# Mixture-of-experts stage: the partner rows of a group's remainder tile are fetched one expert later

## The chip, the cores and the metric

One core of a Trainium2 chip runs the whole program. The metric is the device time of one execution in microseconds (us). A core has five engines that each run their own instruction queue in order and wait for each other by semaphores: TensorE (PE), VectorE (DVE), ScalarE (ACT), GpSimd (POOL) and SyncE (SP). SP and POOL also issue DMA transfers.

## The reference, cut to what matters

One encoder layer over 2048 tokens of width 1024: an input projection, a state-space mixer beside a cross-attention, an output projection, a layer norm, and a mixture of experts with a second layer norm. The change lies in the mixture of experts. Each token picks one of 4 groups and in it 2 of 4 experts; an expert is a gated feed-forward network of width 256.

```python
def _hier_moe(x, wg, bg, we, be, w_gate, w_up, w_down):
    ...
    gsel = jnp.argmax(gl, axis=-1)
    ...
    top_v, top_i = lax.top_k(el, MOE_TOPK)
    ew = jax.nn.softmax(top_v, axis=-1) * gw
    eid = gsel[:, None] * MOE_EXPERTS_PER_GROUP + top_i
    gate = jnp.sum(jax.nn.one_hot(eid, MOE_EXPERTS, dtype=f32) * ew[..., None], axis=1)
    h = jax.nn.silu(jnp.einsum('td,edf->tef', t, w_gate)) * jnp.einsum('td,edf->tef', t, w_up)
    y = jnp.einsum('tef,efd->td', h * gate[..., None].astype(h.dtype), w_down)
...
        moe = _hier_moe(x, router_g_w[i], ...)
        x = _layer_norm(DEEPNORM_ALPHA * x + moe, ln2_g[i], ln2_b[i])
```

## The kernel before, in words

The stages ahead of the experts take the first 690 us or so. Then 16 experts run, in 4 groups of 4, in the order 0 to 14, one overflow tile (named `s0`, for rows that found no place), 15. An expert e handles 288 rows: 256 as two tiles of 128 rows, `xg{e}_0` and `xg{e}_1`, and 32 remainder rows. The remainder rows of the 4 experts of a group g share one tile of 128 rows, `xr{g}`.

What happens to a tile, with the names and lines of the profile:

- `fetch`: SP loads the expert's three f32 weight blocks into `raw` (three buffers); ScalarE (`L91`) and VectorE (`L92`) split each into a high and a low f16 part, `wh` and `wl`. POOL gathers the rows of the two tiles from `x1d` in memory by an indirect DMA (`L1201`).
- `columns`: PE transposes the rows (`pt`, `L1458`), ScalarE copies the high part (`xh`, `L1461`), VectorE takes the low part (`xl`, `L1462`).
- `hidden`: gate and up matmuls `pg`, `pu` (three f16 products each, `L108` to `L110`), two halves; `gated` (`L1046` to `L1049`) makes `hh` on ScalarE and `hl` on VectorE.
- `down`: the down matmuls into `py` (three PSUM buffers in all); VectorE adds `py` times the gate into the tile (`L1499`), which frees the PSUM buffer.
- `store` (`L1206`): POOL scatters the tile into a scratch `xs` in memory, so that the token's other expert finds the sum so far. `earlier` (`L1222`): POOL fetches that sum from `xs`.
- `finish`: the layer norm (`norm`) and a scatter to the output (`L1242`).

The remainder rows end apart: `rest_downs(g)` runs their down matmuls, ScalarE copies the result to `gyr{g}`, VectorE adds it into `xr{g}` (`L1518`), POOL stores `xr{g}`. `partner` then fetches the rows' sums from `xs` into `pzr{g}` (one of two buffers `pz`), and `finish` runs `L881` (`pzr` + `gyr`, VectorE), the square (`L886`, ScalarE), `L882` and `L887` (small, VectorE), the power (`rsr`, `L898`, POOL), `L900` and `L901` (VectorE) and the scatter.

In the loop over the experts (`for n_, e in enumerate(order)`) one iteration writes: the fetches for the next expert, the first half of `hidden(e)`, `downs` of the expert before, `columns` of the next, the second half of `hidden(e)`, the `earlier` of this expert's tiles, and then two or three `finish` taken from the front of the list `todo`. So `downs(e)` is written in the iteration of the expert behind e.

What sets the order on the engines: a scheduler reads the program in written order with its dependencies and sorts each engine's instructions by its own model of their times; on the chip each engine runs its list in order. A fetch from `xs` waits for all stores to `xs` that are written ahead of it; stores among themselves, and a store behind a fetch, don't wait. Tiles take their buffers from pools, `xg` and `gyr` from one of nine.

Of the kernel before, what the change touches and what calls it, by code (L numbers as in the profile page):

```python
# [18 lines left out]
P = 128  # L19
# [9 lines left out]
NE = 16  # L29
# [43 lines left out]
class Kern:  # L73
# [1176 lines left out]
    def moe(self):  # L1250
        nc, a = self.nc, self.a
        V = nc.vector
        with ExitStack() as m:
# [13 lines left out]
            rem = self.mk.tile([P, 4, LW], I32, bufs=1, name="idxrem")  # L1267
# [6 lines left out]
            def fetch_overflow(rows, i, nm, static=True):  # L1274
                li = self.mk.tile([P, 2], I32, tag="li", name=f"li{nm}")
                V.tensor_copy(li, rows[:, ds(i, 1)])
                tk = self.mk.tile([OVT, LW], I32, tag="tk", name=f"tk{nm}")
                with self.tc.issue_after(first) if static else ExitStack():
                    self.gather(tk, self.listd, li[:OVT, 0:1])
                W = self.expert_weights(lambda o, s: self.gather(o, s, li[:, 1:2]), nm)  # L1280
                xg = self.mk.tile([P, D], F32, tag="xg", bufs=XG, name=f"xg{nm}")
                self.gather(xg[:OVT], self.x1d, tk[:, 0:1])
                return W, xg, tk
# [4 lines left out]
            def overflow(f, h, nm):  # L1288
                W, xg, tk = f
                gy = self.gated_rows(nm)  # L1290
                self.down(W, *h, 0, OVT, xg, tk.bitcast(F32)[:OVT, 1:2], nm, gy=gy)
                return gy
# [21 lines left out]
            todo = []  # L1314

            def downs(e, W, xg, h):
                if e >= NE:
                    over.append(overflow(W, h, f"s{e - NE}"))
                    return
                g, i = divmod(e, 4)  # L1320
                hh, hl = h
                if e == NE - 1:
                    rest_downs(g)
                if e < EARLY:
                    x = self.xk[e]
                    if i:
                        todo.append((x, self.partner(P, idx[:, e, 0, 2:3], f"{e}_0"), None))
                        x = self.mk.tile([P, D], F32, tag="xg", bufs=XG, name="xg1_0")
                        self.gather(x, self.x1d, idx[:, e, 0, 0:1])
                        V.tensor_tensor(x, x, self.xk[e], op=ALU.add)  # L1330
                    with self.tc.issue_after(first):
                        self.store(x, P, idx[:, e, 0, 3:4])
                for q, (c, x) in enumerate(xg):
                    sums = [self.mk.tile([P, 1], F32, tag=f"sum{h}", bufs=6, name=f"sum{h}_{e}_{c}") for h in range(2)] if i else None
                    self.down(W, hh, hl, q * P, P, x, gate[:, e, c, 1:2], f"{e}_{c}", sums)
                    self.store(x, P, idx[:, e, c, 3:4])
                    if i:
                        todo.append((x, (None, idx[:, e, c, 2:3], f"{e}_{c}"), sums))
                if i == 3:
                    if e < NE - 1:  # L1340
                        rest_downs(g)
                    todo.append((gys.pop(g), self.partner(P, rem[:, g, 2:3], f"r{g}"), None))

            def rest_downs(g):
                left, xr = lefts.pop(g)
                gy = gys[g] = self.gated_rows(f"r{g}")
                self.down_rest(g, left, xr, gy, grem[:, g, 1:2])
                self.store(xr, P, rem[:, g, 3:4])
# [10 lines left out]
            lefts, rests, gys, over, before = {}, {}, {}, [], None  # L1359
# [7 lines left out]
            for n_, e in enumerate(order):  # L1367
                g, i = divmod(e, 4)
# [16 lines left out]
                if before is not None:  # L1385
                    downs(*before)
# [14 lines left out]
                for _ in range(3 if i == 1 else 2):  # L1401
                    if todo:
                        z, pair, sums = todo.pop(0)
                        self.finish(z, pair, HOW2, sums=sums)
                before = e, W, xg, h
            downs(*before)
            todo.append((over[0], self.partner(OVT, fo[2][:, 2:3], "s0"), None))
            for z, pair, sums in todo:
# [7 lines left out]
            with self.tc.If(flag != 0):  # L1416
# [3 lines left out]
                with self.tc.For_i(NSTAT, n, 1) as i:  # L1420
                    f = fetch_overflow(rows, i, "d", False)
# [170 lines left out]
```

## Time and profile before

| what | value |
|---|---|
| median of three runs | 1093.28 us |
| lowest and highest run | 1093.13, 1101.6 us |
| profiled execution | 1091.53 us |
| its span in the trace | 1089.7 us |
| PE busy over the span | 899.5 us (83%) |
| DVE, ACT, POOL busy | 828.3, 540.5, 535.3 us |

The span runs from the first to the last instruction in the trace; "busy" is the time in which an engine executes. A row of a timeline has the start, the duration, the engine, the line, the operation, the operands and, in brackets, how long the engine stood idle just before and what ended that.

### The profile page before, as it was taken

Reading aid. Unit: us, or ns where it says so; the run is one execution under the profiler, and the core shown is the slowest. Engines: PE = TensorE matmul, PEld = TensorE weight load, DVE = VectorE, ACT = ScalarE, POOL = GpSimd, SP = SyncE. Lnnn points to the kernel's source line nnn. Section 1 sums busy time; section 2 is a strip of 40 time slices with the busy share of each in tenths; the row PEclk is TensorE's granted clock in tenths of the full one; section 3 lists DMA queues with packets and bytes.
Section 4 is the critical chain, followed back from the end, with each engine's and each line's share of the span. In section 5 each row is a group of like instructions: output and inputs, shape, how many; then the busy total and the mean of one; then the engine's idle time right before and its main releaser. Section 6 shows DMA issues by size and latency. Waiting matters only on the chain. (4 is left out here: it accounts for less than half of the span.)

```text
span 1089.7 us, 18757 instructions
## 1 busy us (share of the span) xinstructions
PE 899.5 (83%) x7108; PEld 606.8 (56%) x7108; DVE 828.3 (76%) x1636; ACT 540.5 (50%) x1068; POOL 535.3 (49%) x379
## 2 busy tenths in 40 slices
PE   7777599985845999899999888698979987989880
PEld 4444465674734877444554447476657754755540
DVE  7999888969997666483585676467878787878774
ACT  5122243445748776477633312265656554746530
POOL 1475655426663331325945444525444566367454
PEclk9899799999887999999999987899999998999995
DMA  7113355275271422417736331476578669557531
GB/s 253 41 45 117 121 180 202 69 243 168 61 227 46 132 81 77 140 55 267 257 141 116 78 114 64 142 292 227 206 269 319 215 225 334 198 205 233 208 107 65
DMA packets 65199, 178.14 MB, mean 163 GB/s; under 512 B 15121, under 2 KB 33425, under 8 KB 57681
## 3 DMA queue, kind: packets, MB, share of 16 engines
q1 hardware_dynamic: 44800, 128.83, 36.2%
q0 software_dynamic: 20304, 48.07, 12.9%
q8 instruction: 57, 0.93, 0.3%
q14 instruction: 38, 0.30, 0.1%
HBM read 141.95 MB, written 58.49 MB: 184 GB/s over the span
## 5 line engine op out<-in xcount | busy, mean ns | idle before, releaser
L92 DVE SCALAR_TENSOR_TENSOR wl<-raw,wh 128x1024 f16<-128x1024 f32 x82 | 97.8, 1219 | 10.4 <-ACT wh L91 7.9
L91 ACT ACTIVATE wh<-raw 128x1024 f16<-128x1024 f32 x82 | 82.0, 1048 | 24.1 <-PE pg L109 13.8
L109 PE MATMUL pg<-xl,wh 128*128 128x288 f16 (+1 forms) x256 | 73.3, 288 | 3.0 <-DVE xl L1462 2.8
L110 PE MATMUL pg<-xh,wl 128*128 128x288 f16 (+1 forms) x256 | 73.3, 288 | 0.9 <-issue 0.9
L108 PE MATMUL pu<-xh,wh 128*128 128x288 f16 (+1 forms) x256 | 71.8, 283 | 2.4 <-DVE hl L1049 1.9
L108 PE MATMUL pg<-xh,wh 128*128 128x288 f16 (+1 forms) x256 | 73.5, 289 | 0.0
L1206 POOL DMA_INDIRECT xs<-xg,idxall x31 | 38.9, 1256 | 70.2 <-DVE xg L1499 40.9
L110 PE MATMUL pu<-xh,wl 128*128 128x288 f16 (+1 forms) x256 | 71.6, 282 | 1.5 <-issue 1.5
L109 PE MATMUL pu<-xl,wh 128*128 128x288 f16 (+1 forms) x256 | 71.6, 282 | 0.0
L109 PEld LDWEIGHTS <-wh 128*128 128x128 f16 x576 | 58.1, 101 | 19.0 <-issue 5.7
L108 PEld LDWEIGHTS <-wh 128*128 128x128 f16 x576 | 58.3, 101 | 18.5 <-issue 3.5
L110 PEld LDWEIGHTS <-wl 128*128 128x128 f16 x576 | 57.9, 101 | 17.5 <-issue 4.4
L108 PE MATMUL pq<-xh,S 128*128 128x128 f16 x256 | 51.0, 235 | 15.9 <-DVE OT L295 15.9
L743 POOL TENSOR_TENSOR pe<-pe,ri 128x1024 f32<-128x1024 f32 x16 | 30.3, 1895 | 55.5 <-DVE ri L742 38.8
L108 PE MATMUL pu<-winh,xh 128*128 128x512 f16 x128 | 49.7, 388 | 6.6 <-ACT winh L91 6.6
L1201 POOL DMA_INDIRECT xg<-x1d,idxall x31 | 37.9, 1222 | 32.9 <-DMA out_x<-xg,idxall 13.0
L108 PE MATMUL py<-wh,hh 128*128 128x512 f16 x120 | 45.9, 385 | 8.8 <-ACT hh L1048 4.6
L1462 DVE TENSOR_TENSOR xl<-pt,xh 128x512 f16<-128x512 f32 x60 | 39.5, 683 | 16.1 <-ACT xh L1461 10.1
L1461 ACT ACTIVATE xh<-pt 128x512 f16<-128x512 f32 x60 | 34.0, 592 | 35.8 <-PE pt L1458 29.5
L110 PE MATMUL pq<-xh,S 128*128 128x128 f16 x256 | 51.2, 235 | 0.4 <-DVE S L92 0.3
L1458 PE MATMUL pt<-ident,xg 128*128 128x128 f32 x240 | 37.8, 285 | 16.5 <-DVE xl L1462 7.6
L691 POOL TENSOR_TENSOR m<-S,R 128x1024 f32<-128x1024 f32 x10 | 30.4, 3045 | 42.0 <-DVE S L715 23.6
(471 smaller groups left out, 3163.6 us busy)
## 6 DMA issues: line engine op xcount, KB each, us to landing
raw<-in_w_gate SPq DMA_DIRECT2D x16, 1024.0 KB
raw<-in_w_up SPq DMA_DIRECT2D x16, 1024.0 KB
raw<-in_w_down SPq DMA_DIRECT2D x16, 1024.0 KB
xr<-in_xT SPq DMA_DIRECT2D x16, 512.0 KB
xs<-wo SPq DMA_DIRECT2D x16, 512.0 KB
wol<-xs SPq DMA_DIRECT2D x16, 512.0 KB
M<-kd SPq DMA_DIRECT2D x64, 128.0 KB
xres<-in_x SPq DMA_DIRECT2D x16, 512.0 KB
```

Of the source, the lines that this page charges most:

```text
L91: self.nc.scalar.activation(hi, raw, AF.Copy, scale=WS)
L92: self.nc.vector.scalar_tensor_tensor(lo, raw, WS, hi, op0=ALU.mult, op1=ALU.subtract)
L108: mm(ps, lh, rh, start=first, stop=False)
L109: mm(ps, lh, rl, start=False, stop=False)
L110: mm(ps, ll, rh, start=False, stop=last)
L691: Q.tensor_tensor(m[:, 1], S[:, :, 1::-1], tab(1), op=ALU.mult)
L743: nc.gpsimd.tensor_tensor(pe, pe, ri.unsqueeze(2).to_broadcast([P, 4, 256]), op=ALU.mult)
L1201: return self.nc.gpsimd.indirect_dma_start(out=out, out_offset=None, in_=src, in_offset=bass.IndirectOffsetOnAxis(ap=idx, axis=0))
L1206: st = self.nc.gpsimd.indirect_dma_start(out=self.xs, out_offset=bass.IndirectOffsetOnAxis(ap=si, axis=0), in_=z[:sz], in_offset=None, bou ...
L1458: nc.tensor.transpose(pt[:, i, off:off + sz], x[:sz, (d0 + i) * P:(d0 + i) * P + P], self.ident[:sz, :sz])
L1461: nc.scalar.activation(xh[:, ds_, :n], pt, AF.Copy)
L1462: nc.vector.tensor_tensor(xl[:, ds_, :n], pt, xh[:, ds_, :n], op=ALU.subtract)
```

## The change

In `downs` the last expert of a group no longer appends the group's remainder rows to `todo` and no longer fetches their partners. That is done at the end of `downs` of the first expert of the next group, so behind that expert's two stores, and with the index of the group before. The last group, whose last expert is the last of all, keeps its place.

```diff
--- before.py
+++ after.py
@@ -1336,10 +1336,12 @@
                     self.store(x, P, idx[:, e, c, 3:4])
                     if i:
                         todo.append((x, (None, idx[:, e, c, 2:3], f"{e}_{c}"), sums))
-                if i == 3:
-                    if e < NE - 1:
-                        rest_downs(g)
-                    todo.append((gys.pop(g), self.partner(P, rem[:, g, 2:3], f"r{g}"), None))
+                if i == 3 and e < NE - 1:
+                    rest_downs(g)
+
+                if i == 0 and g or e == NE - 1:
+                    r = g if i else g - 1
+                    todo.append((gys.pop(r), self.partner(P, rem[:, r, 2:3], f"r{r}"), None))
 
             def rest_downs(g):
                 left, xr = lefts.pop(g)
```

Both finish the remainder rows of group g in the iteration of expert 4g+5; what is written elsewhere in the program is the fetch. The list of instructions is the same, and up to expert 5's first half all engines have the same order in both. Behind that the scheduler sorts differently; lines behind `L1338` carry a number higher by two in the changed kernel.

VectorE at the boundary of groups 0 and 1 (`pzr0` are the partner rows of group 0, `xg4_0` and `xg4_1` the tiles of expert 4, `wl7_0` a weight of expert 7); before:

```order
L1049 TENSOR_TENSOR hl5_9048<-pu5_0_9050,hh5_9047 128x288
L881 SCALAR_TENSOR_TENSOR pzr0_8898,mur0_9238<-pzr0_8898,gyr0_8841 128x1024
L1499 SCALAR_TENSOR_TENSOR xg4_0_8468<-py4_0_0_9104,idxall_7794,xg4_0_8468 128x512
L1499 SCALAR_TENSOR_TENSOR xg4_0_8468<-py4_0_1_9112,idxall_7794,xg4_0_8468 128x512
L1499 SCALAR_TENSOR_TENSOR xg4_1_8470<-py4_1_0_9123,idxall_7794,xg4_1_8470 128x512
L92 SCALAR_TENSOR_TENSOR wl7_0_9254<-raw7_0_9251,wh7_0_9253 128x1024
L882 TENSOR_SCALAR mur0_9238<-mur0_9238 128x1
```

and after, from the same place, with a piece left out and then where `L881` of `pzr0` is now:

```order
L1049 TENSOR_TENSOR hl5_9044<-pu5_0_9046,hh5_9043 128x288
L1501 SCALAR_TENSOR_TENSOR xg4_0_8468<-py4_0_0_9100,idxall_7794,xg4_0_8468 128x512
L1501 SCALAR_TENSOR_TENSOR xg4_0_8468<-py4_0_1_9108,idxall_7794,xg4_0_8468 128x512
L1501 SCALAR_TENSOR_TENSOR xg4_1_8470<-py4_1_0_9119,idxall_7794,xg4_1_8470 128x512
L92 SCALAR_TENSOR_TENSOR wl7_0_9254<-raw7_0_9251,wh7_0_9253 128x1024 x2
```

```order
L92 SCALAR_TENSOR_TENSOR wl8_0_9504<-raw8_0_9501,wh8_0_9503 128x1024 x2
L881 SCALAR_TENSOR_TENSOR pzr0_9138,mur0_9238<-pzr0_9138,gyr0_8841 128x1024
L92 SCALAR_TENSOR_TENSOR wl8_2_9520<-raw8_2_9517,wh8_2_9519 128x1024
L1501 SCALAR_TENSOR_TENSOR xg5_0_8736,sum0_5_0_9338<-py5_0_0_9340,idxall_7794,xg5_0_8736 128x512
L1501 SCALAR_TENSOR_TENSOR xg5_0_8736,sum1_5_0_9339<-py5_0_1_9348,idxall_7794,xg5_0_8736 128x512
```

`L881` stood ahead of the three `L1499` of expert 4 and now stands 16 rows further down, ahead of those of expert 5.

POOL at the boundary of groups 1 and 2 (`pzr1` are the partner rows of group 1, `xg11_1` a tile of expert 11); before:

```order
L1206 DMA xs_541<-xr1_8573,idxrem_7796 2048x1024
L1201 DMA xg11_0_10332<-x1d_5321,idxall_7794 128x1024
L1206 DMA xs_541<-xg8_0_9525,idxall_7794 2048x1024
L1222 DMA pzr1_9955<-xs_541,idxrem_7796 128x1024
L1201 DMA xr3_10687<-x1d_5321,idxrem_7796 128x1024
L1206 DMA xs_541<-xg8_1_9527,idxall_7794 2048x1024
L1201 DMA xg11_1_10334<-x1d_5321,idxall_7794 128x1024
L1242 DMA out_x<-xg7_1_9277,idxall_7794 2048x1024
```

and after:

```order
L1206 DMA xs_541<-xg8_0_9525,idxall_7794 2048x1024
L1201 DMA xg11_0_10332<-x1d_5321,idxall_7794 128x1024
L1242 DMA out_x<-xg7_1_9277,idxall_7794 2048x1024
L1206 DMA xs_541<-xg8_1_9527,idxall_7794 2048x1024
L1201 DMA xg11_1_10334<-x1d_5321,idxall_7794 128x1024
L1201 DMA xg12_0_10582<-x1d_5321,idxall_7794 128x1024
L1222 DMA pzr1_10195<-xs_541,idxrem_7796 128x1024
L1222 DMA xg9_0_9793<-xs_541,idxall_7794 128x1024
```

The fetch of `pzr1` moved from ahead of the gather of `xg11_1` to behind it and the first gather of expert 12, and the scatter of `xg7_1` moved ahead of that gather.

PE at the same place (`pt11` are the transposed tiles of expert 11, `pg10_1` the second half of expert 10's gate matmuls); before, with one of the transposes that need `xg11_1` at the third row:

```order
L110 MATMUL pu10_0_10341<-xh10_10199,wl10_1_10085 128x288
L1458 MATMUL pt11_2_10446<-ident_60,xg11_0_10332 128x128
L1458 MATMUL pt11_0_10439<-ident_60,xg11_1_10334 128x128
L1458 MATMUL pt11_0_10439<-ident_60,xg11_0_10332 128x128
L1458 MATMUL pt11_0_10439<-ident_60,xg11_1_10334 128x128
L1458 MATMUL pt11_2_10446<-ident_60,xg11_1_10334 128x128
```

and after, the same piece and then where the transposes of `xg11_1` are now:

```order
L110 MATMUL pu10_0_10341<-xh10_10199,wl10_1_10081 128x288
L1460 MATMUL pt11_2_10446<-ident_60,xg11_0_10332 128x128
L110 LDWEIGHTS hl9_10101
L110 MATMUL py9_0_0_10397<-wh9_2_9787,hl9_10101 128x512
L110 LDWEIGHTS hl9_10101
```

```order
L108 LDWEIGHTS wh10_0_10072
L108 MATMUL pg10_1_10467<-xh10_10199,wh10_0_10072 128x288
L1460 MATMUL pt11_0_10439<-ident_60,xg11_1_10334 128x128
L1460 MATMUL pt11_0_10439<-ident_60,xg11_0_10332 128x128
L1460 MATMUL pt11_0_10439<-ident_60,xg11_1_10334 128x128
```

Three down matmuls of expert 9 and 19 gate matmuls of expert 10 stand ahead of the transposes of `xg11_1` that used to stand behind them.

VectorE at the boundary of groups 2 and 3 (`xl14` belongs to expert 14, `hl13` to 13, `xls0` to the overflow tile); before:

```order
L1462 TENSOR_TENSOR xl14_11258<-pt14_4_11273,xh14_11257 128x2x256
L92 SCALAR_TENSOR_TENSOR wls0_2_11389<-raws0_2_11386,whs0_2_11388 128x1024 x2
L881 SCALAR_TENSOR_TENSOR pzr2_11013,mur2_11353<-pzr2_11013,gyr2_10956 128x1024
L1462 TENSOR_TENSOR xl14_11258<-pt14_6_11280,xh14_11257 128x2x256
L1049 TENSOR_TENSOR hl13_11163<-pu13_1_11288,hh13_11162 128x288
L1462 TENSOR_TENSOR xls0_11498<-pts0_0_11499,xhs0_11497 128x4x64
```

and after:

```order
L1464 TENSOR_TENSOR xl14_11258<-pt14_4_11273,xh14_11257 128x2x256
L1464 TENSOR_TENSOR xl14_11258<-pt14_6_11280,xh14_11257 128x2x256
L1049 TENSOR_TENSOR hl13_11159<-pu13_1_11288,hh13_11158 128x288
L881 SCALAR_TENSOR_TENSOR pzr2_11253,mur2_11353<-pzr2_11253,gyr2_10956 128x1024
L1464 TENSOR_TENSOR xls0_11498<-pts0_0_11499,xhs0_11497 128x4x64
```

`L881` of `pzr2` moved two rows down, behind `xl14` and `hl13`, and stays ahead of `xls0` and of the `L1501` of expert 13. On POOL the fetch of `pzr2` moved behind the store of `xg12_1`, two scatters to the output and a gather, ahead of the fetch of `xg13_0`.

## Rows read from the trace of the kernel before

**Rows 1.** The page, its first line.
```profile
span 1089.7 us, 18757 instructions
```

**Rows 2.** Windows: from:to and length, busy PE, PEld, DVE, ACT, POOL, clock, DMA share, GB/s.
```profile
core 0: us, PE busy (x) PEld busy (x) DVE busy (x) ACT busy (x) POOL busy (x), PEclk, DMA share, GB/s
694.00:1060.00 366.00, 321.99 (x2479) 225.37 (x2476) 288.02 (x446) 204.04 (x357) 188.12 (x154) 0.96 0.68 236
830.00:880.00 50.00, 48.63 (x362) 35.93 (x361) 41.06 (x66) 31.74 (x56) 25.08 (x20) 1.00 0.67 231
930.00:980.00 50.00, 45.63 (x324) 32.56 (x325) 41.60 (x71) 29.80 (x52) 23.77 (x20) 0.97 0.60 206
816.10:820.00 3.90, 3.90 (x14) 1.84 (x14) 3.90 (x6) 1.36 (x3) 2.66 (x3) 0.56 0.73 217
919.80:925.60 5.80, 5.80 (x25) 4.14 (x26) 3.05 (x5) 2.77 (x6) 3.16 (x4) 0.50 0.85 331
1021.00:1024.00 3.00, 2.64 (x11) 0.97 (x10) 3.00 (x8) 0.48 (x2) 2.35 (x2) 0.53 0.14 48
```

**Rows 3.** Timelines of POOL, DVE and PE at the boundary of groups 0 and 1.
```profile
809.97 1.04 POOL L1222 DMA_INDIRECT pzr<-xs,idxrem  x1 [3.65 <-DMA xs<-xr,idxrem]
814.14 1.23 DVE L881 SCALAR_TENSOR_TENSOR pzr<-pzr,gyr 128x1024 f32<-128x1024 f32 x1 [6.57 <-DMA pzr<-xs,idxrem]
816.09 0.38 PE L108 MATMUL py<-wh,hh 128*128 128x512 f16 x1 [3.40 <-DVE xg L1499]
```

**Rows 4.** Groups by line: count, ns of one (mean, or least, median, most).
```profile
L92 DVE SCALAR_TENSOR_TENSOR wl<-raw,wh 128x1024 f16<-128x1024 f32 x82 | 97.8, 1219 | 10.4 <-ACT wh L91 7.9
L881 DVE SCALAR_TENSOR_TENSOR pzr<-pzr,gyr x4: 1217/1222/1226, 814.1 to 1068.3; 128x1024 f32<-128x1024 f32 x4
L886 ACT ACTIVATE junkr<-pzr,mur x4: 1139/1148/1149, 818.6 to 1071.1; 128x1024 f16<-128x1024 f32 x4
L900 DVE SCALAR_TENSOR_TENSOR pzr<-pzr,mur,g x4: 1274/1276/1277, 821.5 to 1072.4; 128x1024 f32<-128x1024 f32 x4
```

**Rows 5.** Timelines of POOL and PE at the boundary of groups 1 and 2.
```profile
902.39 1.03 POOL L1222 DMA_INDIRECT pzr<-xs,idxrem  x1 [0.39 <-issue]
910.53 0.95 POOL L1201 DMA_INDIRECT xg<-x1d,idxall  x1 [2.53 <-DMA xs<-xg,idxall]
911.79 2.66 POOL L1242 DMA_INDIRECT out_x<-xg,idxall  x1 [0.30 <-issue]
907.54 0.28 PE L108 MATMUL pu<-xh,wh 128*128 128x288 f16 x1 [1.86 <-DVE hl L1049]
919.78 1.54 PE L1458 MATMUL pt<-ident,xg 128*128 128x128 f32 x6 [5.63 <-DMA xg<-x1d,idxall]
```

**Rows 6.** Timeline of PE, first and last of 48 gate and up matmuls.
```profile
1012.91 0.29 PE L108 MATMUL pg<-xh,wh 128*128 128x288 f16 x1
1018.67 0.29 PE L110 MATMUL pu<-xh,wl 128*128 128x288 f16 x1
```

**Rows 7.** Timelines of POOL, DVE and PE at the boundary of groups 2 and 3.
```profile
999.85 2.05 POOL L1222 DMA_INDIRECT pzr<-xs,idxrem  x1 [0.20 <-issue]
1002.21 1.92 POOL L1206 DMA_INDIRECT xs<-xg,idxall  x1 [0.30 <-DVE wls L92]
1014.98 1.02 POOL L1222 DMA_INDIRECT xg<-xs,idxall  x1 [8.07 <-DMA xs<-xg,idxall]
1019.20 1.28 DVE L901 SCALAR_TENSOR_TENSOR pzr<-pzr,rsr,b 128x1024 f32<-128x1024 f32 x1 [4.54 <-POOL rsr L898]
1006.39 0.39 PE L108 MATMUL py<-wh,hh 128*128 128x512 f16 x1 [1.70 <-ACT hh L1048]
1020.90 0.19 PE L108 MATMUL pgs<-xhs,whs 128*128 128x64 f16 x1 [1.95 <-DVE hl L1049]
```

**Rows 8.** Timeline of PE, two waits behind the boundary of groups 1 and 2.
```profile
955.43 0.28 PE L109 MATMUL pg<-xl,wh 128*128 128x288 f16 x1 [1.79 <-DVE xl L1462]
973.03 0.81 PE L1458 MATMUL pt<-ident,xg 128*128 128x128 f32 x4 [2.57 <-DVE xl L1462]
```

## The prediction, made before the changed kernel ran

> **What bounds the kernel now.** I read the page first, then the stage table, then the timelines of the queues at each group boundary. The page gives the span, 1089.7 us [rows 1]; the profiled execution took 1091.53 us, so 1.83 us lie around the span, and it is 1.75 us under the median of the runs shown, 1093.28. The sum below is made against 1091.53 and moved to the median at the end.
>
> The diff touches only the expert stage, 694 to 1060 us in the stage table [rows 2]. There TensorE (PE) is busy for 322.0 of 366 us and VectorE (DVE) for 288.0, ScalarE and GpSimd (POOL) for 204 and 188. So PE paces the stage, and what a change can give back is PE's idle 44 us, and the time in which PE runs at a lower clock after an idle stretch. On every engine the order of both kernels is the same up to the first group boundary at about 807 us, and the last group's partner fetch is left alone. Three places remain: the boundaries of groups 0/1, 1/2 and 2/3.
>
> **Boundary 0/1, where the wait is plain.** On POOL the partner fetch waits 3.65 us until the store of the remainder rows has landed, and is issued at 809.97. VectorE stands at `L881` for 6.57 us until the rows are there, at 814.14 [rows 3]. Behind `L881` on VectorE stand the three `L1499` that empty PSUM buffers of expert 4's output (three `py` buffers in all), so PE stands at its next down matmul for 3.40 us, until 816.09 [rows 3]. And after that the granted clock is 0.56 for 3.9 us [rows 2], near the 1.2 GHz of the two levels 1.2 and 2.4: 3.9 x 0.44 = 1.7 us lost. This place costs PE 3.40 + 1.7 = 5.1 us.
>
> After the change VectorE goes from `hl5` straight to the `L1499` of expert 4 (order above), whose matmuls are done, since PE is what waits for them. I take the whole 5.1 back: **-5.1**. Bounds: 0 (another wait of that size ends at the same place) and -6.6 (VectorE's whole stall). The three long VectorE instructions of the finish, 1.22 + 1.28 + 1.28 = 3.8 us [rows 4, 7], don't go away: they now lie in 830 to 880.
>
> **Boundary 1/2.** PE stands 5.63 us at the transposes of `xg11_1` until 919.78, and before that 1.86 us for `hl` [rows 5]; then the clock is 0.50 for 5.8 us [rows 2], 2.9 us lost: 10.4 us in all. The gather of `xg11_1` was issued at 910.53, after POOL waited 2.53 us for a store, and landed 9.25 us later [rows 5]. The partner fetch is not what POOL waits for there: it waited only 0.39 us [rows 5]. The change takes it out from ahead of this gather (1.03 + 0.39 = 1.4 us) and puts the scatter of `xg7_1` there (2.66 + 0.30 = 3.0 us), of which the 2.53 us of waiting take up most: 1.4 + 2.53 - 3.0 = 0.9 us earlier. On PE it puts 19 gate matmuls of expert 10 and three down matmuls ahead of the transposes that wait. 48 gate and up matmuls took from 1012.91 to 1018.67 [rows 6], 0.123 us each; the 512-column ones I scale to 0.22: 19 x 0.123 + 3 x 0.22 = 3.0 us. So 3.9 of the 5.63 are covered, and with a shorter idle stretch I count half of the 2.9 lost to the clock: -3.9 - 1.5 = **-5.4**. Bounds: 0 (the gather lands as much later as it is better covered) and -10.4 (all of it).
>
> The Trainium skill, page "DMA: Bandwidth & Descriptors", section "Anatomy of one DMA — SWDGE (gpsimd) path", gives a DMA as about 2.0 us plus its bytes over 436 GB/s, an estimate of 3.2 us for these 512 KB. The fetch of `pzr` agrees: 811.01 to 814.14, 3.13 us [rows 3]. The gather of `xg11_1` does not: 9.25 us [rows 5], with a DMA share of 0.85 right behind it [rows 2]. By the page the wait here would vanish with any cover over a few us, and this boundary would give 8.5 instead of 5.4; by the rows it is queueing, and only the part that is covered goes.
>
> **Boundary 2/3.** PE loses 1.70 us (waiting for ScalarE's `hh`), 1.95 us (for `hl`) [rows 7] and 3.0 x 0.47 = 1.4 us of clock after it [rows 2]: 5.05. VectorE's own stall, 4.54 us at `L901`, comes from POOL: the small `rsr` stands behind the fetch of `xg13_0`, which waits 8.07 us for the store of `xg12_1` [rows 7]. That store was issued at 1002.21 and had landed by 1014.98.
>
> Now the partner fetch itself stands behind that store (a fetch waits for every store to the scratch that is written ahead of it in the program, and expert 12's two now are). The store goes out 2.3 us earlier, since the fetch with its 2.05 us is no longer ahead of it, so it lands at about 1012.6; fetch issue 1.0 and flight 3.1 bring the rows at about 1016.7, and `L881`, the square on ScalarE and `L900` (1.22, 1.15 and 1.28 [rows 4], with some 0.3 around them) end at about 1020.7, and only then come the `L1499` of expert 13. On PE, `py13_1_1` needs one of them and stands 24 gate and 6 up matmuls after 1012.91, at about 1016.6 (30 x 0.123). A wait of about 4 us plus some clock takes the place of 1.95 + 1.4; against it, the third part of the overflow expert's weights is gathered about 1.2 us earlier (one gather less ahead of it on POOL, 0.95 + 0.30 by the nearest row [rows 5]), which shortens the 1.70. I take **0**, bounds -5 (all gone) and +6.6 (a stall like the one of 0/1, which this is nearest to).
>
> **What is given back.** The 3.8 us of finish move twice into stretches in which VectorE is 41.1 and 41.6 of 50 us busy [rows 2]: 82 and 83% become about 90%. PE is 97% busy in the first, so its next work is rarely late by more than one instruction of 1.2 us; in the second PE already waits for `xl` (1.79 and 2.57 us [rows 8]) and a longer queue lengthens such waits. I take +1 for each, **+2**; bounds 0 (both lie in idle time) and +7.6 (every us of them is on the path). No instruction is added or removed, and transfers are the same; SP's queue keeps its order, so the weight loads move only with the buffers they wait for, at nothing in the sum (ScalarE's and VectorE's splits are what releases them, and both have idle time).
>
> **Sum.** -5.1 - 5.4 + 0 + 2 = -8.5: the profiled execution from 1091.5 to 1083.0, the median from 1093.3 to **about 1084.8 us**, 0.8% faster.
>
> **The rivals.** A measurement of this kernel tells about 1% from no change, here 1082.3 and 1104.2.
>
> *Given back (B).* The boundary waits go, but PE, 88% busy, meets another late operand soon after: a `xl` or a freed PSUM buffer that VectorE reaches 3.8 us later, or the same gathers landing no sooner. For it: the stage's waits have several releasers, and the transposes wait for transfers whose queueing the change does not touch. Against it: at 0/1 nothing but `L881` was late. Gain: the 5.1 of 0/1 less up to 5: 1088 to 1093.
>
> *The late fetch blocks VectorE (C, the other side).* A fetch that waits for three stores instead of one can be later than the place that the schedule gives `L881`, and VectorE, which runs in order, then stands there. Place: 2/3 above all, and 0/1 and 1/2 in their new places if the rows come after VectorE arrives. Price: a stall like the present one, PE waiting 3.4 to 5.6 plus 1.7 to 2.9 of clock, 5.1 to 8.5 at each boundary. It decides when the store of the next group's first expert lands more than about 5 us after VectorE is through the work ahead of `L881`; the 8.07 us POOL waits for such a store [rows 7] speak for it, the 16 rows put ahead of `L881` at 0/1, eight splits of 1.22 us among them [rows 4], against it. With 0/1 stalled as now in another place (0), nothing gained at 1/2 (0), 6.6 more at 2/3 and 2 given back it is +8.6, about 1102; from 1097 (0/1 gained after all) to 1107 (8.5 in place of 5.1 at 0/1, and 8.5 more at 2/3).
>
> The Trainium skill speaks for C: the same page, section "Rules for kernel authors", wants the DMA issued early, and its semaphore waited for late. Here only the second half is done, and the first is undone; the trace of before shows the price of waiting too soon, 6.57 us [rows 3], and no row shows that of issuing later.
>
> *All of it comes back (D).* If at 1/2 and 2/3 the waits go with their clock, it is -5.1 - 10.4 - 5 + 2 = -18.5, or -13 if half of 1/2's remainder stays: 1072 to 1080, about 1075.
>
> **Chances.** Forecast (gains 4 to 13, 1080 to 1089) 0.50; B 0.20; C 0.15; D 0.15. Two fifths of the first and all of D lie under 1082.3: faster 0.35. A little under half of C lies over 1104.2: slower 0.07. Within 1%: 0.58. The range 1075 to 1098 leaves out half of D and most of C, about 0.2; the likeliest case's own is 1080 to 1089.
>
> **What would show it.** Step one is right if the 6.57 us at `L881` and PE's 3.40 us at 816 are gone and the clock there stays near 1. Step two: PE's wait at the transposes of `xg11_1` at 2 us or under, the gather issued about 1 us earlier. Step three: at about 1010 to 1020 VectorE idle at `L881` for some 5 us, and PE waiting for `L1501` of expert 13. Given back: VectorE near 90% in the 50 us behind the first two boundaries, with PE's waits for `xl` longer by about 1 us each. The prediction is wrong if `L881` stalls VectorE at 0/1 or 1/2 in its new place, or if the gathers of tiles land later because fetches now crowd them.

## The result, and the profile after

| | before | changed |
|---|---|---|
| median of 15 runs | 1093.13 us | 1104.04 us |
| ratio | | 1.0100 (1.0078 to 1.0121) |
| span of the profiled execution | 1089.7 us | 1099.7 us |

The change costs 1.0%, 10.9 us by the medians, where 0.8% of gain was forecast, and the time lies above the range.

The first line of the page and the windows of the changed kernel, columns as in [rows 2]:

```profile
span 1099.7 us, 18769 instructions
694.00:1060.00 366.00, 311.54 (x2404) 220.72 (x2404) 284.56 (x435) 198.08 (x349) 195.37 (x151) 0.94 0.66 233
804.00:830.00 26.00, 26.00 (x197) 19.36 (x195) 17.48 (x23) 15.09 (x25) 10.78 (x9) 1.00 0.85 300
```

The 12 instructions more than in [rows 1] are waits for semaphores. In the same 366 us PE is busy for 10.5 us less than in [rows 2]. The boundary 0/1 (second window) is what the first step of the prediction said: PE never idle, clock 1.00, where it had 3.90 us at 0.56. VectorE's timeline there, against the stall of 6.57 us in [rows 3]:

```profile
806.15 2.07 DVE L1501 SCALAR_TENSOR_TENSOR xg<-py,idxall,xg 128x512 f32<-128x512 f32 x3 [2.94 <-PE py L110]
828.51 1.22 DVE L881 SCALAR_TENSOR_TENSOR pzr<-pzr,gyr 128x1024 f32<-128x1024 f32 x1
```

VectorE is now ahead of PE at the first row, and `L881` of group 0 finds its rows in place. Where the time went, in PE's timeline of the changed kernel:

```profile
851.57 1.11 PE L1460 MATMUL pt<-ident,xg 128*128 128x128 f32 x4 [3.57 <-DVE xl L1464]
861.08 0.38 PE L108 MATMUL py<-wh,hh 128*128 128x512 f16 x1 [1.73 <-DVE xg L1501]
919.94 0.44 PE L1460 MATMUL pt<-ident,xg 128*128 128x128 f32 x1 [10.07 <-DMA xg<-x1d,idxall]
1020.37 0.66 PE L1460 MATMUL pts<-ident,xgs 64*128 64x64 f32 x4 [9.28 <-DMA xgs<-x1d,tks]
```

Two new long waits, both for gathers: 10.07 us for `xg11_1` (5.63 in [rows 5]) and 9.28 us for the overflow tile `xgs0` (none before). The first two rows stand for five waits of 0.75 to 3.57 us between 851 and 883, 9.4 us together; before, PE had one of 1.3 us there.

A yardstick that needs no alignment of the two traces is the time from the store of one group's remainder tile (`L1206 xs<-xr`) to the next one's:

| from store to store | xr0 to xr1 | xr1 to xr2 | xr2 to xr3 |
|---|---|---|---|
| before | 93.4 | 96.1 | 64.7 |
| changed | 92.8 | 100.7 | 74.3 |

One profile of the same stretch varies by up to 7 us; the experiments below give further profiles with the same order in a stretch.

### The profile page after: what moved, and what is told of

It is laid out like the page before. It is cut to its first block, busy times and chain, and to the rows that moved or that the text cites. A ratio compares the mean times of both kernels' runs of the same rounds, so it can differ in the third digit from the quotient of the medians.

```text
span 1099.7 us, 18769 instructions
## 1 busy us (share of the span) xinstructions
PE 894.9 (81%) x7108; PEld 601.6 (55%) x7108; DVE 831.2 (76%) x1636; ACT 539.5 (49%) x1068; POOL 547.9 (50%) x379
## 5 line engine op out<-in xcount | busy, mean ns | idle before, releaser
L1206 POOL DMA_INDIRECT xs<-xg,idxall x31 | 38.5, 1241 | 54.7 <-DVE xg L1501 21.1
L108 PE MATMUL pq<-xh,S 128*128 128x128 f16 x256 | 49.2, 231 | 16.7 <-DVE OT L295 16.7
L691 POOL TENSOR_TENSOR m<-S,R 128x1024 f32<-128x1024 f32 x10 | 34.1, 3406 | 41.9 <-DVE S L715 23.6
L1501 DVE SCALAR_TENSOR_TENSOR xg<-py,idxall,xg 128x512 f32<-128x512 f32 x60 | 43.2, 742 | 9.7 <-PE py L110 4.9
L110 PE MATMUL pu<-winh,xl 128*128 128x512 f16 x128 | 49.3, 385 | 0.5 <-POOL xl L262 0.5
L109 PE MATMUL pu<-winl,xh 128*128 128x512 f16 x128 | 49.3, 385 | 0.1
```

The lines of the kernel that those rows point to most:

```text
L108: mm(ps, lh, rh, start=first, stop=False)
L109: mm(ps, lh, rl, start=False, stop=False)
L110: mm(ps, ll, rh, start=False, stop=last)
L691: Q.tensor_tensor(m[:, 1], S[:, :, 1::-1], tab(1), op=ALU.mult)
L1206: st = self.nc.gpsimd.indirect_dma_start(out=self.xs, out_offset=bass.IndirectOffsetOnAxis(ap=si, axis=0), in_=z[:sz], in_offset=None, bou ...
L1501: nc.vector.scalar_tensor_tensor(xg[:sz, hs], py[:sz], gate, xg[:sz, hs], op0=ALU.mult, op1=ALU.add, **acc)
```

## The experiments

### Which boundary, and is it the fetch?

Four kernels fetch late only for some groups. The edit, with the set of groups changed from kernel to kernel:

```diff
-                if i == 0 and g or e == NE - 1:
+                late = (0,)
+                if i == 0 and g - 1 in late or i == 3 and g not in late:
```

`late0`:

> Only group 0's partner rows are fetched late; groups 1 to 3 as before. The changed kernel took 1104.0 us against 1093.1. Theory Q (the loss comes from POOL's one queue being sorted anew: scatters and gathers that wait stand ahead of what PE needs): this kernel has at the boundary 1/2 the same sorting as the changed kernel (the two scatters of expert 7 and the gather of xr3 ahead of the store of xg8_1), but at 2/3 the gather of xgs0 is where it was, so it pays about 4 to 5 us at 1/2 and nothing at 2/3, with the 5 us gained at 0/1 given back by 890 us: about 1097 us. Theory F (each late fetch is paid where it stands, since its rows come late to L881): groups 1 and 2 are as before, so no loss at 1/2 and 2/3: about 1093 or, with the gain of 0/1, 1088 us.

Measured: 1.0040 of before (1.0015 to 1.0064).

`late1`:

> Only group 1's partner rows are fetched late. POOL's order at 1/2 is that of before without the fetch of pzr1, which stands behind the scatter of xg7_1; at 2/3 xgs0 is gathered early. Theory Q: the gather of xg11_1 comes 1 to 2 us earlier than before, no new wait: 1089 to 1093 us, L881 of group 0 still stalls VectorE for 6.6 us. Theory F: the late fetch of group 1 costs what the changed kernel lost between its stores of xr1 and xr2, 4.6 us: about 1098 us.

Measured: 1.0038 (1.0008 to 1.0067).

`late2`:

> Only group 2's partner rows are fetched late; up to that boundary all queues are those of before, and xgs0 is gathered ahead of the store of xg12_0 as before. Theory Q: the changed kernel lost 9.6 us behind the store of xr2 because xgs0 is gathered behind two scatters; here it is not, so 1092 to 1096 us (the fetch behind the store of xg12_1 may stall L881 by some us, partly hidden). Theory F: the 9.6 us come from the late fetch of pzr2 itself: about 1102 us.

Measured: 1.0005 (0.9985 to 1.0025).

`late01`:

> Groups 0 and 1 are fetched late, group 2 as before. POOL's order at 1/2 and at 2/3 is that of the changed kernel (xgs0 behind the two scatters of expert 11), except that pzr2 is fetched ahead of the store of xg12_1. Theory Q: the whole loss stays: 1102 to 1106 us, with PE waiting some 9 us for xgs0. Theory F: without the late fetch of group 2 the 9.6 us are gone: about 1094 us.

Measured: 1.0128 (1.0076 to 1.0180).

Rows of PE's timelines: one each of `late0`, `late1` and `late2`, and two of `late01`, in this order:

```profile
924.72 0.45 PE L1461 MATMUL pt<-ident,xg 128*128 128x128 f32 x1 [8.35 <-DMA xg<-x1d,idxall]
```

```profile
923.68 0.69 PE L1461 MATMUL pt<-ident,xg 128*128 128x128 f32 x2 [5.55 <-DMA xg<-x1d,idxall]
```

```profile
917.44 0.90 PE L1461 MATMUL pt<-ident,xg 128*128 128x128 f32 x3 [5.27 <-DMA xg<-x1d,idxall]
```

```profile
920.85 0.45 PE L1461 MATMUL pt<-ident,xg 128*128 128x128 f32 x1 [10.82 <-DMA xg<-x1d,idxall]
1021.82 0.44 PE L1461 MATMUL pts<-ident,xgs 64*128 64x64 f32 x2 [7.21 <-DMA xgs<-x1d,tks]
```

The long wait for `xg11_1` comes with the late fetch of group 0 (8.35, 10.82, 10.07), not with that of group 1 or of group 2 alone (5.55 and 5.27; before 5.63). The wait for `xgs0` is there without a late fetch of group 2 (`late01`), and absent where only one group is late. So the two large losses fall at later boundaries than the fetches that bring them, as theory Q says, and the late fetch of group 2 alone costs nothing that the measurement shows. `late1` missed what Q expected (no loss) and came out near what F expected, 1098 us; its loss of 0.4%, in an interval that reaches down to 0.1%, is not explained. Part of its profile's length lies at boundary 0/1, where all engines still have the order of before, and PE stood 9.49 us instead of 3.40 [rows 3]:

```profile
818.87 0.59 PE L108 MATMUL py<-wh,hh 128*128 128x512 f16 x1 [9.49 <-DVE xg L1502]
```

### What the order does

POOL's timeline shows where the two gathers lose their time. In the changed kernel, between the store of `xr1` and the gather of `xg11_1` (one small instruction left out):

```profile
892.27 4.09 POOL L1206 DMA_INDIRECT xs<-xr,idxrem  x1 [3.75 <-DVE xr L1520]
896.67 1.91 POOL L1242 DMA_INDIRECT out_x<-xg,idxall  x1 [0.30 <-DVE xg L1501]
...
901.91 1.91 POOL L1201 DMA_INDIRECT xr<-x1d,idxrem  x1 [2.73 <-DMA xs<-xr,idxrem]
904.13 2.61 POOL L1206 DMA_INDIRECT xs<-xg,idxall  x1 [0.30 <-issue]
907.05 1.18 POOL L1201 DMA_INDIRECT xg<-x1d,idxall  x1 [0.30 <-issue]
908.53 3.17 POOL L1242 DMA_INDIRECT out_x<-xg,idxall  x1 [0.30 <-issue]
912.00 0.99 POOL L1206 DMA_INDIRECT xs<-xg,idxall  x1 [0.30 <-issue]
916.88 0.98 POOL L1201 DMA_INDIRECT xg<-x1d,idxall  x1 [3.90 <-DMA xs<-xg,idxall]
```

`xg11_1` takes the buffer of `xg8_0` and can only be gathered when the store of that tile (904.13) has landed, in the last row. Ahead of that store stand a slow issue (4.09), a scatter (1.91) and the gather of `xr3`, which waits 2.73 us for the store of `xr1` and takes 1.91: from the store of `xr1` to that of `xg8_0` it is 11.9 us, and to the gather 24.6. In POOL's timeline of before only the gather of `xg11_0` stood between them, and that of `xr3` came behind:

```profile
896.93 0.98 POOL L1206 DMA_INDIRECT xs<-xr,idxrem  x1 [2.29 <-DVE xr L1518]
898.22 2.21 POOL L1201 DMA_INDIRECT xg<-x1d,idxall  x1 [0.30 <-issue]
900.74 1.26 POOL L1206 DMA_INDIRECT xs<-xg,idxall  x1 [0.30 <-issue]
903.73 1.91 POOL L1201 DMA_INDIRECT xr<-x1d,idxrem  x1 [0.31 <-issue]
```

It was 3.8 us (896.93 to 900.74), and 13.6 to the gather at 910.53 [rows 5]. Of the 11 us more, 8.1 lie ahead of the store, 3.0 behind it. Not all of them reach PE: behind its issue the gather took 2.1 us until PE went on (917.86 to 919.94), before 8.3 (911.48 to 919.78). Counted from the store of `xr1`, PE has the tile 27.7 us later in the changed kernel and 22.9 us later before, a difference of 4.8 us. The same view at 2/3:

```profile
999.20 1.77 POOL L1206 DMA_INDIRECT xs<-xg,idxall  x1 [0.18 <-issue]
1001.28 3.46 POOL L1242 DMA_INDIRECT out_x<-xg,idxall  x1 [0.30 <-issue]
1005.04 4.60 POOL L1242 DMA_INDIRECT out_x<-xg,idxall  x1 [0.30 <-issue]
1009.95 0.92 POOL L1201 DMA_INDIRECT xgs<-x1d,tks  x1 [0.30 <-issue]
1011.17 1.03 POOL L1222 DMA_INDIRECT pzr<-xs,idxrem  x1 [0.30 <-issue]
```

`xgs0` is issued behind two scatters of 3.46 and 4.60 us and lands 9.5 us after its issue has ended; before it was issued ahead of the store of `xg12_0`:

```profile
994.65 0.92 POOL L1201 DMA_INDIRECT xgs<-x1d,tks  x1 [0.30 <-issue]
998.04 1.00 POOL L1206 DMA_INDIRECT xs<-xg,idxall  x1 [0.30 <-issue]
```

Its place hangs on a buffer (with one of its own, in `a_xgs` below, it moves ahead again): in the programs `xgs0` lies where `xg11_0` was (before) and where `xg12_0` was (changed). `gyr0`, held longer, passes its buffer to `xg9_0` instead of `xg8_0`, and the tiles behind it turn to other ones.

Two kernels set one of these places at a time. `b_pin23` is the kernel before with one edge more (here and in the next two cuts the lines that keep an instruction for later use are left out):

```diff
-                self.gather(xg[:OVT], self.x1d, tk[:, 0:1])
+                with self.tc.issue_after(self.outs["11_1"]) if static else ExitStack():
+                    self.gather(xg[:OVT], self.x1d, tk[:, 0:1])
```

> The kernel before with one edge: the gather of xgs0 is issued behind the scatter of xg11_1 (where the changed kernel has it, there behind two scatters); nothing is fetched later, all else stands as before. If xgs0's place in POOL's queue is what costs at 2/3: PE waits 5 to 9 us for xgs0, 1098 to 1103 us. If it is only a sign of something else (DMA load, the partner fetch): within 2 us of before.

Measured: 1.0085 (1.0052 to 1.0119), and PE's timeline has the wait:

```profile
1015.00 0.66 PE L1461 MATMUL pts<-ident,xgs 64*128 64x64 f32 x4 [8.43 <-DMA xgs<-x1d,tks]
```

The place of this one gather, with nothing fetched later, brings a wait of the changed kernel's size (9.28).

`a_xrlate` is the changed kernel with another place for the gathers of the remainder tiles:

```diff
-                return xr, self.gather(xr, self.x1d, rem[:, g, 0:1])
+                with self.tc.issue_after(self.stores[4 * g - 4, 1]) if g > 1 else ExitStack():
+                    return xr, self.gather(xr, self.x1d, rem[:, g, 0:1])
```

> The changed kernel with the gather of a group's remainder tile (xr2, xr3) issued behind the store of the second tile of the group's... first expert before it (xg4_1, xg8_1), so that POOL does not stand at it (3.9 and 2.7 us in the changed kernel) ahead of that store. If this waiting is what delays the gather of xg11_1: PE's wait there falls from 10 to about 6 us and the time by some 4 us, to 1100. If the gather is late for its buffer alone: 10 us and 1104 stay. The wait for xgs0 (9 us) stays in both.

Measured: 1.0069 (1.0041 to 1.0097), 0.3% under the changed kernel's ratio, with intervals that overlap; from the store of `xr1` to that of `xr2` its profile took 93.0 us instead of 100.7. Its waits:

```profile
924.69 0.69 PE L1463 MATMUL pt<-ident,xg 128*128 128x128 f32 x2 [3.60 <-DMA xg<-x1d,idxall]
1018.54 0.66 PE L1463 MATMUL pts<-ident,xgs 64*128 64x64 f32 x4 [9.53 <-DMA xgs<-x1d,tks]
```

10.07 has become 3.60, and the wait for `xgs0` stays, as expected of the order. The edge moved more than the gather of `xr3`: in this program the scatter of `xg7_0` and the gather of `xg11_0` are back where they were before. So it shows what the order ahead of the store of `xg8_0` costs, not the share of the one gather.

### Taking the two losses away

`a_xgs` gives `xgs0` a buffer of its own:

```diff
-PZ = 2
+PZ = 1
-                xg = self.mk.tile([P, D], F32, tag="xg", bufs=XG, name=f"xg{nm}")
+                xg = self.mk.tile([P, D], F32, tag="xgs" if static else "xg", bufs=1 if static else XG, name=f"xg{nm}")
```

and takes the partner rows of `s0` into a tile buffer (that edit is left out here), since there is one `pz` left.

> The changed kernel, but xgs0 has a buffer of its own (room for it: one partner buffer less, and the overflow tile's partner rows in a tile buffer). The order at 0/1 and 1/2 is the changed kernel's, pzr2 is fetched behind the same two scatters; only the gather of xgs0 has moved ahead. Theory R (at 2/3 the loss is xgs0's buffer and place in the queue): no wait for xgs0, some 7 us less than the changed kernel, so 3 to 5 us above before. Theory F (the late pzr2 stalls VectorE there anyway): as slow as the changed kernel, 10 us above before, with PE waiting for VectorE instead.

Measured: 1.0045 (1.0019 to 1.0071). There is no wait for `xgs0`; in its place PE waits for VectorE, behind the `L881` that stands for the late `pzr2`:

```profile
1023.76 0.38 PE L108 MATMUL py<-wh,hh 128*128 128x512 f16 x1 [4.57 <-DVE xg L1504]
1021.04 1.23 DVE L881 SCALAR_TENSOR_TENSOR pzr<-pzr,gyr 128x1024 f32<-128x1024 f32 x1 [8.14 <-DMA pzr<-xs,idxrem]
```

That is not a price of the late fetch alone. In `late1`, where `pzr2` is fetched early, PE waits as long at the same matmuls, behind a VectorE that stands at `L901` for the small `rsr` (as in [rows 7]):

```profile
1029.13 0.59 PE L108 MATMUL py<-wh,hh 128*128 128x512 f16 x1 [5.02 <-DVE xg L1502]
1024.85 1.28 DVE L901 SCALAR_TENSOR_TENSOR pzr<-pzr,rsr,b 128x1024 f32<-128x1024 f32 x1 [6.64 <-POOL rsr L898]
```

`a_fix` has both repairs, the edits of `a_xrlate` and `a_xgs`.

> Both repairs: xgs0 with its own buffer, and the gathers of xr2 and xr3 behind the stores of xg4_1 and xg8_1. If the two account for the loss: within 3 us of before, and faster than before if the 5 us of boundary 0/1 were still in it. If the late fetch costs by itself: 5 us or more above before.

Measured: 1.0012 (0.9982 to 1.0041). With both repairs the loss is gone, within the measurement; but the gain at 0/1 doesn't appear either. In its profile xr1 to xr2 took 92.0 us, 8.7 less than in the changed kernel, and xr2 to xr3 72.0, only 2.3 less. That last stretch took 68 to 72 us in all eight kernels with one `pz` (these two and six below), whether `pzr2` was fetched early or late; whether the one `pz` is the reason was not tried.

Stretches with the same order in several kernels can be set side by side (us from store to store, one profile each):

| stretch | order of before | order of the changed kernel |
|---|---|---|
| xr0 to xr1 | 93.4, 95.0, 96.4, 97.2 | 92.8, 97.6, 91.0 |
| xr1 to xr2 | 96.1, 95.8, 92.7 | 100.7, 101.4, 98.0 |
| xr2 to xr3 | 64.7, 67.0, 68.0, 66.7 | 74.3, 74.2, 75.1, 75.8 |

First row: before, late2, b_pin23, late1; changed, late0, late01. Second: before, late2, b_pin23; changed, late01, a_xgs. Third, by the place of `xgs0` alone, with other differences in the order: before, late2, late1, late0; changed, b_pin23, late01, a_xrlate. The means differ by 93.8 - 95.5 = -1.7, 100.0 - 94.9 = +5.1 and 74.9 - 66.6 = +8.3: together +11.7, near the 10.9 of the medians. The first difference is smaller than the spread of its profiles.

### Is there a cost of the fetch itself?

`finlate` fetches where the kernel before does and only queues the finish later (cut to the lines that matter):

```diff
+                    fetched[g] = gys.pop(g), self.partner(P, rem[:, g, 2:3], f"r{g}"), None
+                if i == 1 and g or e == NE - 1:
+                    todo.append(fetched.pop(g if i == 3 else g - 1))
```

> The other half of the change: the partner rows are fetched where they were (last expert of the group), and only their finish is queued later, behind the second expert of the next group. gyr and the partner buffer are held longer. If issuing early and waiting late is what pays: L881 stalls nowhere, 3 to 6 us faster than before. If holding gyr longer is what costs (the tile buffers turn, POOL is sorted anew): 3 to 10 us slower than before, without any late fetch.

Measured: 1.0079 (1.0051 to 1.0107). No fetch is later and `L881` stalls at no boundary, and it is as slow as the second of the two expectations says: a later finish, which holds `gyr` and the partner buffer longer, is enough for a loss. But it is not the loss of the changed kernel. In `finlate` the finish is written two experts later than in both others (`L881` of group 0 runs at 842.2 us; 814.1 before, 828.5 changed), and PE's waits are others: for `xg11_1` it stands about as long as before, for `xgs0` not at all, and longest for `xl`:

```profile
922.48 0.90 PE L1461 MATMUL pt<-ident,xg 128*128 128x128 f32 x3 [5.04 <-DMA xg<-x1d,idxall]
857.13 1.11 PE L1461 MATMUL pt<-ident,xg 128*128 128x128 f32 x4 [5.89 <-DVE xl L1465]
```

The next pair holds the buffers fixed: `gyr` of groups 0 to 2 gets one of its own, for which one `pz` goes.

```diff
-        return self.mk.tile([P, D], F32, tag="xg", bufs=XG, name=f"gy{nm}")
+        own = nm in ("r0", "r1", "r2")
+        return self.mk.tile([P, D], F32, tag="gy" if own else "xg", bufs=1 if own else XG, name=f"gy{nm}")
```

`b_owngyr`, with the early fetch:

> The kernel before, but gyr of groups 0 to 2 gets a buffer of its own instead of one of the nine of the tiles (room for it: one partner buffer instead of two). It is the pair of the next kernel, with the same buffers for every tile. Both theories: within some us of before, 1085 to 1096 us, since one tile buffer more is free.

Measured: 1.0048 (1.0024 to 1.0072); from the last remainder matmul to the end of the last scatter's issue it took 34.1 us instead of 25.0, since with one `pz` two fetches at the end follow each other.

`a_owngyr`, the same with the late fetch:

> The same with the late fetch of the changed kernel. Every tile has the same buffer as in its pair, so a later end of gyr can't move xg or xgs0 to another buffer. Theory R (the loss comes from the buffers: gyr is held longer, the tiles behind it turn to other buffers, xgs0 gets that of xg12_0 instead of xg11_0, and POOL's queue is sorted accordingly): no wait for xgs0, and against its pair -6 to +3 us. Theory F (fetching late costs by itself): +8 to +12 us against its pair.

Measured: 1.0178 (1.0133 to 1.0223), so 1.3% over its pair: theory R failed here. The stretches xr1 to xr2 and xr2 to xr3 were as it said (94.6 and 68.4, its pair 95.2 and 70.6), but xr0 to xr1 took 113.5 us against 92.4, in a profile of the slowest of its four runs. POOL's timeline has the place:

```profile
801.61 1.75 POOL L1243 DMA_INDIRECT out_x<-xg,idxall  x1 [0.59 <-DVE xg L901]
812.46 0.97 POOL L1201 DMA_INDIRECT xg<-x1d,idxall  x1 [9.11 <-DMA out_x<-xg,idxall]
813.74 5.44 POOL L1206 DMA_INDIRECT xs<-xg,idxall  x1 [0.30 <-DVE xg L1502]
```

The gather of `xg8_0`, a tile of expert 8 while expert 5 is computed, stands 9.11 us until a scatter has landed, ahead of the stores of expert 4, for which the fetches of `pzr0` and of expert 5 wait. In its pair the store of `xg4_0` stands ahead of that gather.

Three more runs test this, with the longer end mended (the partner rows of `s0` in a tile buffer). `b_best` has the early fetch:

> The kernel before with gyr of groups 0 to 2 in a buffer of its own, one partner buffer, and the overflow tile's partner rows in a tile buffer, so that the end of the program need not wait for the one partner buffer (that made the last 34 us of the earlier run of this kind 9 us longer). The fetch is early. In that run VectorE did not stall at L881 of group 0 and the stretch from one remainder tile's matmuls to the next took 92 us instead of 100 to 105. If that holds, 1 to 8 us faster than before; if it was chance, as before.

Measured: 0.9950 (0.9929 to 0.9971), faster than both kernels. `L881` of group 0 waits 0.54 us, but that of group 1, which found its rows in place before, now waits 6.24:

```profile
807.53 1.23 DVE L881 SCALAR_TENSOR_TENSOR pzr<-pzr,gyr 128x1024 f32<-128x1024 f32 x1 [0.54 <-DMA pzr<-xs,idxrem]
908.30 1.23 DVE L881 SCALAR_TENSOR_TENSOR pzr<-pzr,gyr 128x1024 f32<-128x1024 f32 x1 [6.24 <-DMA pzr<-xs,idxrem]
```

PE has no wait of 1 us or more for a gather in this profile behind 795 us, where it had 5.63 for `xg11_1` [rows 5].

`a_best`, `a_best0` and `a_best12` fetch late for all three groups, for group 0, and for groups 1 and 2 (the `late` of the first edit):

> The late fetch of the changed kernel, with gyr of groups 0 to 2 in its own buffer, as a pair to the fastest kernel so far (the same with the early fetch: 0.5% under before). The earlier pair of this kind differed by 1.3%, all of it in its profile between the remainder matmuls of groups 0 and 1 (109 against 92 us), where POOL stands 9 us at the gather of xg8_0 ahead of the stores of xg4. If that is the rule: again 10 to 15 us above its pair, 1098 to 1103. If it was chance: within 4 us of its pair.

> The same, fetched late for group 0 alone. Theory O (order: only where the late fetch lets the scheduler put a waiting gather ahead of the stores is it dear, which is at 0/1 alone): as slow as with all three late, 1097 to 1103. Theory F (each late fetch costs its share): a third, some 1092.

> The same, fetched late for groups 1 and 2 alone; the tile buffers are those of the pair, and POOL's queue there has no gather that waits ahead of the stores. Theory O: within 3 us of the pair, 1086 to 1092. Theory F: two thirds of the loss, 1095 to 1099.

Measured: 1.0067 (1.0041 to 1.0093), 1.0125 (1.0089 to 1.0161) and 0.9984 (0.9964 to 1.0004). POOL's wait at `xg8_0` in `a_best` and `a_best0`:

```profile
811.01 0.97 POOL L1201 DMA_INDIRECT xg<-x1d,idxall  x1 [8.68 <-DMA out_x<-xg,idxall]
```

```profile
811.20 0.98 POOL L1201 DMA_INDIRECT xg<-x1d,idxall  x1 [8.06 <-DMA out_x<-xg,idxall]
```

From xr0 to xr1 they took 109.2 and 111.6 us, `a_best12`, with POOL's order of `b_best` there, 92.2 and `b_best` 91.7. Group 0 alone is at least as dear as all three, and the other two cost 0.3% against `b_best`, some 3.7 us and a little more than theory O allowed, with intervals that overlap. So a late fetch has at most a small price of its own, and a large one at 0/1, where a waiting gather stands ahead of stores in all three slow kernels. That this gather is the cause is argued from the rows: no run kept the late fetch and put the gather back. Why `a_best0` is slower than `a_best` is not settled.

## Why the prediction was wrong

**Boundary 0/1: the mechanism was right, keeping the gain was not.** The stall of 6.57 us, PE's 3.40 and the low clock are gone. But the stretch is 1.7 us shorter by the means, not 5.1, and that is within its spread. PE comes earlier to work whose operands don't: VectorE's timeline has, one expert on, first before and then in the changed kernel,

```profile
864.85 0.75 DVE L1499 SCALAR_TENSOR_TENSOR xg<-py,idxall,xg 128x512 f32<-128x512 f32 x1 [1.19 <-DMA xg<-xs,idxall]
870.89 1.28 DVE L900 SCALAR_TENSOR_TENSOR xg<-xg,mu,g 128x1024 f32<-128x1024 f32 x1 [2.72 <-DMA xs<-xg,idxall]
```

```profile
860.27 0.75 DVE L1501 SCALAR_TENSOR_TENSOR xg<-py,idxall,xg 128x512 f32<-128x512 f32 x1 [2.44 <-DMA xg<-xs,idxall]
868.52 1.28 DVE L900 SCALAR_TENSOR_TENSOR xg<-xg,mu,g 128x1024 f32<-128x1024 f32 x1 [4.29 <-DMA xs<-xg,idxall]
```

In these profiles VectorE waits 2.8 us longer for a fetched sum and for a store to land, and PE waits for VectorE. That is rival B at this place; that the round of store and fetch sets the pace there is read from these rows, and no run took it away.

**Boundary 1/2: the step that failed is "0.9 us earlier".** It priced only what moved between the gather of `xg11_1` and its neighbours. The 2.53 us [rows 5] are a wait for the store of `xg8_0`, and that store itself came 8.1 us later: the gather of `xr3`, whose wait for the store of `xr1` other issues had covered, now stands with a scatter between the two stores. So the gather is issued 11.0 us later, counted from the store of `xr1`, instead of 0.9 earlier, and the tile is there 4.8 us later; the 3.0 us of matmuls put ahead of the transposes are more than used up: +5.1 for the stretch instead of -5.4. The landing was not sized well either: the prediction's 9.25 us are counted from the start of the issue, its 3.13 us of the fetch from the end of one. From the end both ways it is 8.3 against 3.13, and in the changed kernel 2.1.

**Boundary 2/3: a term was missing.** The forecast stall at `L881` came, and longer than the 5 us or so that were to show it:

```profile
1020.46 1.23 DVE L881 SCALAR_TENSOR_TENSOR pzr<-pzr,gyr 128x1024 f32<-128x1024 f32 x1 [10.10 <-DMA pzr<-xs,idxrem]
```

But it runs beside PE's wait for `xgs0`, which ends at 1020.37, and PE did not wait for `L1501` behind it. The gather of `xgs0` behind two scatters, which stood in the order (the "gather" that the fetch of `pzr2` moved behind), got no price; the sum even counted its move as a gain, since it no longer stood ahead of the overflow weights (the 1.2 us). It cost 8.3 us.

**Given back** was put at +2 for VectorE's busier stretches; no run separates it from the waits above. VectorE was busy for 38.8 and 44.0 us of the two stretches of 50 us, not for about 45 in both.

**Rivals.** The time, 1104.0, is in the range of C, and C named 2/3, but that it fits is luck: VectorE did stand 10.10 us at `L881` of group 2 in the changed kernel, but `late2`, which has that fetch late and stands 6.51 us there, loses nothing that shows, so the stall was not what decided. The Trainium skill, page "DMA: Bandwidth & Descriptors", section "Rules for kernel authors", asks for issuing early and waiting late. `finlate` did both and lost 0.8%: with buffers that come from one pool, waiting late also means holding longer. With the buffer out of the pool, issuing early agrees with it: `b_best` at 0.9950 against 1.0067 for its pair `a_best`.

```profile
1016.14 1.23 DVE L881 SCALAR_TENSOR_TENSOR pzr<-pzr,gyr 128x1024 f32<-128x1024 f32 x1 [6.51 <-DMA pzr<-xs,idxrem]
```

## What to carry to other kernels

A wait removed from one in-order queue is worth its size only if nothing else on that path is due soon; and a tile held longer can move the tiles behind it in its pool to other buffers, and with them the order of the queue that gathers them. Before a moved fetch is priced, list the moving queue up to the next thing that the pacing engine needs, with every wait in it, also one and two stages on. When a long-held tile shares a rotating pool, try a buffer of its own first: here, with one partner buffer less and the overflow tile's partner rows moved, it took away the stall at 0/1 that the change was aimed at, and the kernel was 0.5% faster.

## What the runs showed of the hardware

The issue of an indirect DMA on POOL took 0.9 to 5.4 us for the same 512 KB form (0.98 and 5.44 in the rows above), and a scatter in front of an urgent gather can cost 4.6 us by its issue alone (the second scatter ahead of `xgs0`). From the end of the issue to the instruction that waited for it, 512 KB took 3.1 us for `pzr0` before [rows 3], 8.3 for `xg11_1` before and 2.1 for the same tile in the changed kernel, and the 256 KB of `xgs0` there 9.5. In these four stretches the DMA share was 0.70, 1.0, 0.86 and 1.0: the two long ones fell where the DMA engines were busy throughout, which no run varied by itself. Two profiles of the same instructions at the same place differed by 6 us in one stall (3.40 in [rows 3], 9.49 in `late1`), so a stage is to be judged by several profiles.
